# A long convolution's second transform in four 64x64 quarters of TensorE, and its spectral product taken from PSUM

## The chip, the cores and the metric

One core of a Trainium2 chip runs the whole kernel. The metric is the device time of one execution in microseconds (us); several executions are timed and the median is quoted. A core has five engines that work side by side, each through its own instructions in order: TensorE (PE, with its weight loads shown apart as PEld), VectorE (DVE), ScalarE (ACT), GpSimd (POOL) and SyncE (SP), which here issues nearly all DMA transfers. PE writes its results into PSUM, 8 banks of 128 partitions x 512 f32 numbers; DVE and ACT read them there. Semaphores make an engine wait for another.

## The reference, cut to what matters

The block has attention heads and Hyena heads side by side, then a mixture of experts. The Hyena part is what changes: a long convolution of length 2 x 2048 by FFT, twice (two orders), on 512 channels.

```
Hf = rfft(filters, n=2L)                      # per order, per channel, complex
z = v
for o, gate in enumerate((x1, x2)):
    Z = rfft(z, n=2L)
    y = irfft(Z * Hf[o], n=2L)[:L]            # complex product per frequency
    z = gate * (y + z * bias[o])
```

## The kernel before, in words

**Two sides.** `block_kernel` builds a left side (input projection, then attention) and a right side (filters, Hyena, a part of a later embedding), both as Python generators that yield a declared cost. `interleave` draws from the side that is behind by those costs, so the costs set the order in which instructions are handed over. The tile framework then sets each engine's order. As engines take their instructions in order, a matmul of the right side that waits also holds the left side's matmuls behind it.

**FFT in matmuls.** The transform of 4096 points is split in 128 x 32. Step one multiplies with a 128x128 matrix (`w1`) and writes to a DRAM scratch (`s_f` for filters, `s_z` for data); it is read back with other partitions (`zt`). Step two has 32 matrices of 128x128 (`w2[j]`), one matmul each for 128 channels. Each of these matrices is sparse: two residues (halves) with real and imaginary rows.

**Filter stage** (`stage_filter`), 8 rounds (2 orders x 4 channel blocks): `gen` makes 32 slices of a filter in 8 calls of 8 matmuls of 64x64x128 and DVE multiplies by a decay window; `norm` scales; `fft1` is step one (8 calls); `fft2` is step two (8 calls of 4 matmuls), whose results ACT copies from PSUM and SP stores to `h_f`, real and imaginary part twice each, as the product needs them. Three PSUM banks in rotation (`psm`, tag `pm`) serve all four.

**Hyena stage** (`stage_hyena`), pairs of channel blocks in turn: `step1` (step one), then `mid` 8 times per order and block: load `zt` and the filter `ab`, four matmuls with `w2` (L503), ACT copies the result to `zf` (L505), two DMAs swap its upper and lower 64 partitions into `zs` (L507, L508), because the real part needs the imaginary one; DVE multiplies both (L509, L510), POOL adds (L511), four matmuls go back with `wa` (L514), ACT copies (L516), SP stores to `t_z`. `back` reads `t_z`, multiplies with `wb` and the gate, and feeds `step1` of the second order. Two PSUM banks, `ph0` and `ph1`, serve these.

**Around it.** L149 to L151 are the input projection's matmuls, L210 and L213 its short convolution on DVE. In attention L725 makes scores for a maximum (DVE reduces it, L727), L790 and L793 are the scores, L803 is the product with v, L813 the sums of exponentials. When the Hyena and the embedding part (L1506 to L1524) have given back their PSUM, attention gets a further bank (`banks_free`, two units of attention later).

Of the kernel before, what the change touches and what calls it, by code (L numbers as in the profile page):

```python
# [8 lines left out]
F32 = mybir.dt.float32  # L9
# [5 lines left out]
ALU = mybir.AluOpType  # L15
AX = mybir.AxisListType
PSUM = bass.MemoryType.PSUM

P = 128
# [264 lines left out]

TWO_PI = 2.0 * math.pi
# [7 lines left out]
def stage_filter(K, st, cns, consts, w_f1, b_f1, freq1, w_f2, b_f2, freq2, w_f3, bias, h_d, s_d):  # L293
# [5 lines left out]
    pc, psm = pool("fi_c", 1), pool("fi_p", 3, space=PSUM)  # L299
# [4 lines left out]
    H2 = (slice(0, 64), slice(64, 128))  # L304
# [8 lines left out]
    zr = pc.tile([1, P], F32, name="zr")  # L313
    nc.vector.memset(zr, 0.0)
# [46 lines left out]
    def gen(o, b, st):  # L361

        cs = slice(b * P, (b + 1) * P)
        st["g"], part = [], pw.tile([P, 8, P], F32, tag="part", name="part", bufs=1)
        st["part"] = part
        for q in range(8):
            dec = pw.tile([P, 4, P], F32, tag="dec", name="dec")
            nc.sync.dma_start(dec, decay_c[:, q * 4:q * 4 + 4, cs])
            ps = psm.tile([P, 512], F32, tag="pm", name="ps")
            hs = H2[q % 2]  # L370
            for i in range(4):
                for d_ in range(2):
                    nc.tensor.matmul(ps[d_ * 64:(d_ + 1) * 64, i * P:(i + 1) * P],
                                     h2[hs, q // 2 * 4 + i, d_ * 64:(d_ + 1) * 64], w3[hs, o, d_, cs],
                                     start=True, stop=True, skip_group_check=True)
            gq = pw.tile([P, 4, P], F32, tag="g", name="g", bufs=GB)
            nc.vector.tensor_tensor(out=gq, in0=ps.rearrange("p (a c) -> p a c", a=4), in1=dec, op=ALU.mult)
            nc.vector.tensor_reduce(out=part[:, q], in_=gq.rearrange("p a c -> p c a"), axis=AX.X, op=ALU.add,
                                    apply_absolute_value=True)
            st["g"].append(gq)  # L380
            yield 0.8
# [49 lines left out]
    def fft2(o, b):  # L431
        for q in range(8):
            js = slice(q * 4, q * 4 + 4)
            zt = pw.tile([P, 4, P], F32, tag="z2", name="zt")
            nc.sync.dma_start(zt, s_d[o, b].rearrange("(j r) n c -> (r n) j c", r=4)[:, js])
            ps = psm.tile([P, 512], F32, tag="pm", name="ps")
            for i in range(4):
                nc.tensor.matmul(ps[:, i * P:(i + 1) * P], K.w2[:, q * 4 + i], zt[:, i], start=True, stop=True)
            hs = pw.tile([P, 4, P], F32, tag="hs", name="hs")
            nc.scalar.copy(hs, ps.rearrange("p (a c) -> p a c", a=4))  # L440
# [3 lines left out]
            if q == 0:  # L444

                nc.sync.dma_start(h_d[o, b, 64:65, 0, 0], hs[64:65, 0])
                nc.sync.dma_start(h_d[o, b, 0:1, 0, 1], zr)
                nc.sync.dma_start(h_d[o, b, 64:65, 0, 1], zr)
            yield 0.9
# [17 lines left out]
def stage_hyena(K, st, wa_c, uc_d, h_d, s_d, t_d, yh_d):  # L467
# [4 lines left out]
    wa = pc.tile([P, 32, P], F32, name="wa")  # L472
# [3 lines left out]
    ps_tile = lambda i: psa.tile([P, 512], F32, tag=f"ph{i}", name="ph")  # L476
    v4 = lambda t: t.rearrange("p (a c) -> p a c", a=4)
    fl = lambda t: t.rearrange("p a c -> p (a c)")
    H2 = (slice(0, 64), slice(64, 128))

    def step1(o, b, z, q):

        for i in range(2):
            ps = ps_tile(i)
            nc.tensor.matmul(ps, K.w1d[H2[i]], fl(z[H2[i]]), start=True, stop=True)
            sg = pw.tile([P, 4, P], F32, tag="s1", name="sg")
            nc.scalar.copy(sg, v4(ps))
            nc.sync.dma_start(s_d[o, b, :, q * 8 + i * 4:q * 8 + i * 4 + 4], sg)
# [6 lines left out]
    def mid(o, b, q):  # L495
        js = slice(q * 4, q * 4 + 4)
        zt = pw.tile([P, 4, P], F32, tag="zt", name="zt")
        nc.sync.dma_start(zt, s_d[o, b].rearrange("(j r) n c -> (r n) j c", r=4)[:, js])
        ab = pw.tile([P, 4, 2, P], F32, tag="ab", name="ab", bufs=HB)
        nc.sync.dma_start(ab, h_d[o, b, :, js])  # L500
        ps = ps_tile(0)
        for i in range(4):
            nc.tensor.matmul(ps[:, i * P:(i + 1) * P], K.w2[:, q * 4 + i], zt[:, i], start=True, stop=True)  # L503
        zf = pw.tile([P, 4, P], F32, tag="zf", name="zf")
        nc.scalar.copy(zf, v4(ps))  # L505
        zs = pw.tile([P, 4, P], F32, tag="zs", name="zs")
# [5 lines left out]
        ps = ps_tile(1)  # L512
        for i in range(4):
            nc.tensor.matmul(ps[:, i * P:(i + 1) * P], wa[:, q * 4 + i], zs[:, i], start=True, stop=True)  # L514
        sg = pw.tile([P, 4, P], F32, tag="s2", name="sg")
        nc.scalar.copy(sg, v4(ps))  # L516
        nc.sync.dma_start(t_d[o, b].rearrange("(j r) n c -> (r n) j c", r=4)[:, js], sg)

    def back(o, b, q):
        bt = pw.tile([P, 8, P], F32, tag="bt", name="bt")  # L520
# [3 lines left out]
        ps = ps_tile(q % 2)  # L524
# [14 lines left out]
    def block(b):  # L539
# [6 lines left out]
        for o in range(2):  # L546
            for q in range(8):
                mid(o, b, q)
                yield 1.8
# [19 lines left out]
def hyena_consts(K, pool, tmp, w1_c, w2_c, wb_c):  # L569
# [4 lines left out]
    K.w2 = pool.tile([P, 32, P], F32, name="w2")  # L574
# [4 lines left out]
    K.sgn = pool.tile([P, 1], F32, name="sgn")  # L579
    nc.vector.memset(K.sgn[0:64], -1.0)  # L580
    nc.vector.memset(K.sgn[64:128], 1.0)
# [26 lines left out]
class Attention:  # L608
# [4 lines left out]
    H2 = (slice(0, 64), slice(64, 128))  # L613
# [1056 lines left out]
def dft_consts():  # L1670
# [53 lines left out]
    w2 = np.ascontiguousarray(w2.transpose(1, 0, 2))  # L1724
    wa = np.ascontiguousarray(wa.transpose(1, 0, 2))
# [42 lines left out]
def block_kernel(tc, A, out):  # L1768
# [4 lines left out]
    h_f = dt("h_f", (2, 4, P, 32, 2, P))  # L1773
# [104 lines left out]
```

## Time and profile before

| | us |
|---|---|
| median of 3 runs | 3211.95 (3210.45 to 3221.18) |
| the profiled execution | 3218.25 |
| its span | 3216.5 |
| PE busy | 2973.7 (92%) |
| DVE busy | 2146.4 (67%) |
| ACT busy | 1401.8 (44%) |
| POOL busy | 1289.7 (40%) |

The profiled execution is 6.3 us above the median, so a sum made in its span is compared with 3218.25 and then moved down by 6.3 us. Busy time of an engine is the union of its instructions. An f32 matmul of the program appears as two records of MATMUL (and two of LDWEIGHTS), so that 8 matmuls are "x16". The form "64*64 64x128" is rows*columns of the array that the matmul uses, and the moving operand. The filter stage lies between 88 and 740 us, the Hyena between 745 and 1511 us.

### The profile page before, as it was taken

How to read it: one execution, taken by the hardware profiler on the slowest of the kernel's cores; microseconds unless marked ns; L12 is line 12 of the kernel's file. 1: busy time of each engine (PE TensorE's matmuls, PEld its weight loads, DVE VectorE, ACT ScalarE, POOL GpSimd, SP SyncE). 2: the span in 40 equal slices, each digit the busy share in tenths (PEclk: the TensorE clock that was granted, in tenths of full speed). 3: DMA queues.
4: the chain of work that ended last, by engine and by line, in shares of the span. 5: the costliest groups of instructions: out<-in, count | busy, mean ns of one | idle time of the engine just before them, and what ended most of it. 6: DMA issues, size and time to landing. Idle time of an engine off the chain costs nothing.

```text
span 3216.5 us, 46830 instructions
## 1 busy us (share of the span) xinstructions
PE 2973.7 (92%) x16505; PEld 2031.9 (63%) x16505; DVE 2146.4 (67%) x2837; ACT 1401.8 (44%) x2200; POOL 1289.7 (40%) x1138
## 2 busy tenths in 40 slices
PE   6989989899899999999899999989999999998897
PEld 5767777685645445354444378866667677675676
DVE  5775675735678768677777745366667676775655
ACT  3243343343344344443444422245556665664322
POOL 1333444424367657565687733101111121121443
PEclk8999989999899999998999999989999999999898
DMA  6468676787856667476100244287789888897553
GB/s 207 132 194 252 202 210 203 209 232 217 253 160 190 196 193 198 149 209 198 62 18 15 60 144 151 98 273 277 250 277 355 290 301 283 295 347 243 183 184 111
DMA packets 549838, 645.08 MB, mean 201 GB/s; under 512 B 68710, under 2 KB 372649, under 8 KB 549215
## 3 DMA queue, kind: packets, MB, share of 16 engines
q1 hardware_dynamic: 529486, 586.58, 57.6%
q0 software_dynamic: 20112, 55.47, 5.4%
q8 instruction: 131, 2.15, 0.3%
q14 instruction: 109, 0.89, 0.1%
HBM read 463.49 MB, written 161.58 MB: 194 GB/s over the span
## 4 chain that ended last, share of the span: by engine, by line
PE 59%; DMA 14%; DVE 10%; issue 4%; POOL 3%; ACT 2%; SPq 1%; DVEq 0%; POOLq 0%; ACTq 0%
PE po L803 5%; PE ps L1314 4%; PE ps L1315 4%; PE ps L1316 4%; PE pa L725 3%; PE pr L1320 3%; PE ps L790 3%; PE ps L793 3%; PE ps L149 2%; PE ps L151 2%; PE ps L150 2%; DMA zt<-s_f 2%; DMA zs<-zf 2%; PE ps L1380 2%; PE ps L1382 2%
## 5 line engine op out<-in xcount | busy, mean ns | idle before, releaser
L1298 DVE TENSOR_TENSOR wl<-raw,wh 128x1024 fp32r<-128x1024 f32 x384 | 463.4, 1223 | 195.3 <-ACT wh L1293 184.7
L1293 ACT CAST wh<-raw 128x1024 fp32r<-128x1024 f32 x384 | 399.0, 1051 | 268.9 <-PE ps L1316 94.6
L813 POOL TENSOR_TENSOR sums<-e,sums 128x512 f32<-128x512 f32 x306 | 427.6, 1412 | 103.3 <-ACT e L794 98.9
L794 ACT ACTIVATE e<-ps 128x512 f32<-128x512 f32 x512 | 291.3, 600 | 273.2 <-PE ps L793 232.8
L727 DVE TENSOR_REDUCE mx<-pa 128x1 f32<-128x512 f32 x512 | 330.8, 681 | 90.5 <-PE pa L725 89.6
L803 PE MATMUL po<-e,v 128*64 128x512 f32 x1024 | 291.4, 624 | 0.9 <-ACT e L794 0.9
L1393 POOL DMA_DIRECT2D y_d<-ob x64 | 36.0, 565 | 593.1 <-DVE ob L1392 350.0
L1314 PE MATMUL ps<-wh,xt 128*128 128x512 f32 (+4 forms) x512 | 212.6, 416 | 6.3 <-ACT wh L1293 6.2
L1315 PE MATMUL ps<-wl,xt 128*128 128x512 f32 (+4 forms) x512 | 206.5, 403 | 7.6 <-DVE wl L1298 7.6
L1316 PE MATMUL ps<-wh,xt 128*128 128x512 f32 (+4 forms) x512 | 202.6, 396 | 0.0
L725 PE MATMUL pa<-kst,q 128*128 128x512 f32 x352 | 144.1, 454 | 22.1 <-DVE mx L727 19.0
L149 PE MATMUL ps<-xh,wh 128*128 128x512 f32 x384 | 158.4, 412 | 1.4 <-ACT U L205 1.3
L151 PE MATMUL ps<-xh,wl 128*128 128x512 f32 x384 | 158.0, 411 | 0.5 <-DVE wl L143 0.5
L150 PE MATMUL ps<-xl,wh 128*128 128x512 f32 x384 | 156.7, 408 | 0.0
L790 PE MATMUL ps<-q,kst 128*128 128x512 f32 x352 | 153.6, 436 | 3.3 <-ACT e L794 2.5
L813 DVE TENSOR_TENSOR sums<-e,sums 128x512 f32<-128x512 f32 x110 | 132.1, 1208 | 26.7 <-ACT e L794 25.7
L793 PE MATMUL ps<-q,k 65*128 65x512 f32 x352 | 143.2, 407 | 2.2 <-DMA q<-mr 2.2
L725 PEld LDWEIGHTS pa<-kst,q 128*128 128x128 f32 x352 | 64.1, 192 | 126.1 <-DVE mx L727 68.6
L89 POOL TENSOR_TENSOR wl<-raw,wh 128x2048 fp32r<-128x2048 f32 (+1 forms) x26 | 103.1, 3968 | 98.4 <-ACT wh L139 90.1
L511 POOL TENSOR_TENSOR zs<-zs,ab 128x512 f32<-128x512 f32 x64 | 89.7, 1402 | 96.3 <-DVE zs L510 70.8
L1320 PE MATMUL pr<-raw,xr 128*32 128x128 f32 (+1 forms) x2112 | 125.5, 302 | 0.9 <-DVE ob L1396 0.9
L1314 PEld LDWEIGHTS ps<-wh,xt 128*128 128x128 f32 (+4 forms) x512 | 95.3, 186 | 44.8 <-issue 14.5
(384 smaller groups left out, 7167.1 us busy)
## 6 DMA issues: line engine op xcount, KB each, us to landing
raw<-in_w_gate_dram SPq DMA_DIRECT2D x128, 512.0 KB
raw<-in_w_up_dram SPq DMA_DIRECT2D x128, 512.0 KB
raw<-in_w_down_dram SPq DMA_DIRECT2D x128, 512.0 KB
h_f<-hs SPq DMA_DIRECT2D x256, 128.0 KB
ab<-h_f SPq DMA_DIRECT2D x64, 512.0 KB
raw<-in_w_in_dram SPq DMA_DIRECT2D x30, 1024.0 KB
xt<-in_x_dram SPq DMA_DIRECT2D x32, 512.0 KB
dec<-in_c_decay_dram SPq DMA_DIRECT2D x64, 256.0 KB
```

The source lines that it names most:

```text
L725: nc.tensor.matmul(pa, qh[:, t * P:(t + 1) * P], self.kst[g][:, q * 512:(q + 1) * 512], start=True, stop=True)
L727: nc.vector.tensor_reduce(out=mx[:, t, q:q + 1], in_=pa, axis=AX.X, op=ALU.max)
L790: mm = nc.tensor.matmul(ps, self.kst[g][:, ks], qh[:, ql_s[i]], start=True, stop=False)
L793: last = nc.tensor.matmul(ps, self.k1[g][:, ks], ql[:65, ql_s[i]], start=False, stop=True)
L794: nc.scalar.activation(out=pe[:, i], in_=ps, func=AF.Exp, scale=0.125)
L803: mm = nc.tensor.matmul(po[H2[i]], v[:, kt, g * 64:(g + 1) * 64], pe[:, i], start=(kt == 0), stop=(kt == NT - 1), skip_group_check=True)
L813: acc[j][1].tensor_tensor(out=sums[j], in0=pe[:, i], in1=src, op=ALU.add)
L1293: nc.scalar.copy(hi, raw)
L1298: nc.vector.tensor_tensor(out=lo, in0=raw, in1=hi.bitcast(F32), op=ALU.subtract)
L1314: nc.tensor.matmul(ps[:m], xt[:, k, 0, :m], hv[:, j], start=(k == 0), stop=False)
L1315: nc.tensor.matmul(ps[:m], xt[:, k, 0, :m], lv[:, j], start=False, stop=False)
L1316: nc.tensor.matmul(ps[:m], xt[:, k, 1, :m], hv[:, j], start=False, stop=(k == 7))
```

## The change

Step two and its way back are cut into 64x64 matrices. For each j the two residues' input rows (64 each) go to a 64-column result of their own, and odd j swap the halves, so that four consecutive matmuls use the four quarters of the array (`spread`). The result of input half h stands in bank h of a pair of banks. The result now holds the real part in 32 partitions and the imaginary part in the next 32. `h_f` is stored in this layout, real part twice and imaginary part twice, as rows of 1024 numbers. In `mid` DVE multiplies the PSUM pair with both parts of the filter and writes two products; their exchange and signs are in a doubled inverse matrix (`wa[:, i]`), whose two parts are summed in PSUM by 32 matmuls of 64x64 (`gather_back`). The copy `zf`, the swap by DMA, the signed product and the sum on POOL are gone. `mid` and `fft2` run 4 times on 8 j in place of 8 times on 4.

`gen` handles two slices at once in four quarters. PSUM: the filter stage has one single bank (`psm`) and one pair (`psd`) in place of three banks; the Hyena one pair (`ph`) in place of `ph0` and `ph1`. ACT's copies go over 1024 columns. The declared costs become 0.5 (gen, fft2) and 1.9 per `mid` call.

```
+def spread(nc, ps, w, src, q):
+    for jj in range(4):
+        for odd in range(2):
+            for h in range(2):
+                nc.tensor.matmul(ps[H2[(h + odd) % 2], h, jj * P:(jj + 1) * P], w[H2[h], q * 8 + jj * 2 + odd],
+                                 src[H2[h], jj * 2 + odd], start=True, stop=True, skip_group_check=True)
+def gather_back(nc, ps, w, src, q):
+    for jj in range(4):
+        for i in range(2):
+            for odd in range(2):
+                for h in range(2):
+                    at = (h + odd) % 2
+                    nc.tensor.matmul(ps[H2[h], at, jj * P:(jj + 1) * P], w[H2[at], i, q * 8 + jj * 2 + odd],
+                                     src[H2[at], i, h, jj], start=(i == 0), stop=(i == 1), skip_group_check=True)
...
-    pc, psm = pool("fi_c", 1), pool("fi_p", 3, space=PSUM)
+    pc, psm, psd = pool("fi_c", 1), pool("fi_p", 1, space=PSUM), pool("fi_d", 1, space=PSUM)
...
     def fft2(o, b):
-        for q in range(8):
...
-            for i in range(4):
-                nc.tensor.matmul(ps[:, i * P:(i + 1) * P], K.w2[:, q * 4 + i], zt[:, i], start=True, stop=True)
...
-            for ab in range(2):
-                for half in range(2):
-                    nc.sync.dma_start(h_d[o, b, half * 64:(half + 1) * 64, js, ab], hs[ab * 64:(ab + 1) * 64])
...
+        for q in range(4):
...
+            spread(nc, ps, K.w2, zt, q)
...
+                        nc.sync.dma_start(h_d[o, b, u:u + 32, q, i], hs[r:r + 32].rearrange("p a c -> p (a c)"))
...
     def mid(o, b, q):
...
-        nc.scalar.copy(zf, v4(ps))
...
-        nc.sync.dma_start(zs[0:64], zf[64:128])
-        nc.sync.dma_start(zs[64:128], zf[0:64])
-        nc.vector.tensor_tensor(out=ab[:, :, 0], in0=ab[:, :, 0], in1=zf, op=ALU.mult)
-        nc.vector.scalar_tensor_tensor(out=zs, in0=zs, scalar=K.sgn, in1=ab[:, :, 1], op0=ALU.mult, op1=ALU.mult)
-        nc.gpsimd.tensor_tensor(out=zs, in0=zs, in1=ab[:, :, 0], op=ALU.add)
...
+        if q == 0:
+            nc.sync.dma_start(ab[32:33, 0, :P], h_d[o, b, 32:33, q, 1, :P])
+            for r in (0, 32):
+                nc.gpsimd.memset(ab[r:r + 1, 1, :P], 0.0)
+        ps = banks()
+        spread(nc, ps, K.w2, zt, q)
+        for i in range(2):
+            nc.vector.tensor_tensor(out=ab[:, i], in0=ab[:, i], in1=fl(ps), op=ALU.mult)
+        ps = banks()
+        gather_back(nc, ps, wa, ab.rearrange("p i (h j c) -> p i h j c", h=2, j=4), q)
```

Three places show what this does to PE's order. In the programs' names L295 is `spread`, L308 `gather_back`, L505 `step1`, L545 `back` after the change; L503, L514, L485 and L526 were these before. Attention's L725, L790, L793, L803 are L741, L806, L809, L819 after, and `gen` L373 is L395.

PE in the filter stage before, one round of its calls:

```order
L423 MATMUL ps<-gh,w1h 128x512
L424 MATMUL ps<-gh,w1l 128x512
L425 MATMUL ps<-gl,w1h 128x512
L438 MATMUL ps<-zt,w_552 128x128 x4
L373 MATMUL ps<-w_200,h_199 64x128 x8
```

PE in the filter stage after, at the end of a round:

```order
L295 MATMUL pd<-zt,w_553 64x128 x16
L448 MATMUL ps<-gh,w1h 128x512
L449 MATMUL ps<-gh,w1l 128x512
L295 MATMUL pd<-zt,w_553 64x128 x16
L450 MATMUL ps<-gl,w1h 128x512
```

A call of `spread` now stands for two of L438; two that use the one pair `pd` stand here with two matmuls between them.

PE in the middle of the Hyena before, from the first product of a `mid` to the second:

```order
L503 MATMUL ph<-zt,w_552 128x128 x4
L725 MATMUL pa<-kst_6422,qh 128x512 x2
L790 MATMUL ps<-q_6647,kst_6422 128x512
L793 MATMUL ps<-q_6647,k_6423 128x512
L725 MATMUL pa<-kst_6422,qh 128x512
L790 MATMUL ps<-q_6647,kst_6422 128x512
L793 MATMUL ps<-q_6647,k_6423 128x512
L803 MATMUL po<-e,v 64x512 x2
L514 MATMUL ph<-zs,wa 128x128 x4
```

The same after:

```order
L295 MATMUL ph<-zt,w_553 64x128 x16
L841 MATMUL pa<-sums,sel 32x512 x3
L841 MATMUL pa<-osq,sel 32x512
L741 MATMUL pa<-kst_6461,q_9336 128x512
L806 MATMUL ps<-q_8439,kst_6461 128x512
L741 MATMUL pa<-kst_6461,q_9336 128x512
L809 MATMUL ps<-q_8439,k_6462 128x512
L806 MATMUL ps<-q_8439,kst_6461 128x512
L809 MATMUL ps<-q_8439,k_6462 128x512
L819 MATMUL po<-e,v 64x512 x2
L741 MATMUL pa<-kst_6461,q_9336 128x512
L308 MATMUL ph<-ab,wa 64x128 x32
```

About one step of attention still stands between the two products; half as many pairs of them are left.

PE at the end of the Hyena before:

```order
L526 MATMUL ph<-bt,wb 64x512 x4
L825 MATMUL pa<-osq,sel 32x512
L725 MATMUL pa<-kst_7662,qh 128x512 x4
L526 MATMUL ph<-bt,wb 64x512 x2
L725 MATMUL pa<-kst_7662,qh 128x512 x10
L1506 MATMUL pt<-ident,pr 128x128 x2
L725 MATMUL pa<-kst_7662,qh 128x512
L1521 MATMUL pp<-plh,ph 128x512
L1522 MATMUL pp<-pll,ph 128x512
```

PE at the end of the Hyena after:

```order
L741 MATMUL pa<-kst_7903,q_12580 128x512 x3
L295 MATMUL ph<-zt,w_553 64x128 x16
L741 MATMUL pa<-kst_7903,q_12580 128x512 x2
L308 MATMUL ph<-ab,wa 64x128 x32
L295 MATMUL ph<-zt,w_553 64x128 x16
L308 MATMUL ph<-ab,wa 64x128 x32
L295 MATMUL ph<-zt,w_553 64x128 x16
L308 MATMUL ph<-ab,wa 64x128 x32
L545 MATMUL ph<-bt,wb 64x512 x16
L1522 MATMUL pt<-ident,pr 128x128 x2
L1537 MATMUL pp<-plh,ph 128x512
L1538 MATMUL pp<-pll,ph 128x512
```

The last calls of `mid` and all eight of the last `back` stand after one another with hardly any attention between them; before, attention filled this place. It comes after 224 of attention's 512 matmuls with v (L803, L819 after), before after 288.

## Rows read from the trace of the kernel before

**Rows 1.** The page: busy us of each engine, share, instructions.

```profile
PE 2973.7 (92%) x16505; PEld 2031.9 (63%) x16505; DVE 2146.4 (67%) x2837; ACT 1401.8 (44%) x2200; POOL 1289.7 (40%) x1138
```

**Rows 2.** Stretch, busy us of PE, PEld, DVE, ACT, POOL; clock, DMA share, GB/s.

```profile
88.00:760.00 672.00, 604.36 (x3957) 497.84 (x3956) 428.06 (x483) 245.52 (x403) 266.60 (x262) 0.94 0.72 208
760.00:880.00 120.00, 100.70 (x462) 71.21 (x460) 69.95 (x104) 43.52 (x81) 34.55 (x45) 0.87 0.76 228
880.00:1480.00 600.00, 561.95 (x2551) 292.45 (x2548) 466.99 (x618) 260.86 (x484) 399.43 (x290) 0.99 0.64 185
...
1500.00:1540.00 40.00, 32.47 (x97) 16.89 (x93) 20.71 (x35) 12.12 (x20) 4.40 (x4) 0.79 0.54 168
...
1600.00:1800.00 200.00, 198.01 (x774) 93.70 (x772) 158.81 (x231) 91.36 (x162) 158.35 (x119) 1.00 0.07 16
```

**Rows 3.** The chain of waits by line, 880 to 1480 us.

```profile
by line: PE po L803 12.4%; PE pa L725 8.2%; DMA zs<-zf 7.3%; issue 7.1%; PE ps L790 6.9%; PE ps L793 5.8%; PE ph L503 4.2%; PE ph L514 3.7%; DVE mx L727 3.5%; DVE ab L509 3.3%; DMA ab<-h_f 3.2%; PE ph L485 3.0%; PE ph L526 2.9%; DVE sums L8
```

**Rows 4.** Timeline of PE near 309 us: start, length, line, form, count.

```profile
308.62 0.40 PE L150 MATMUL ps<-xl,wh 128*128 128x512 f32 x1
308.86 0.39 PE L151 MATMUL ps<-xh,wl 128*128 128x512 f32 x1
309.17 1.09 PE L373 MATMUL ps<-w,h 64*64 64x128 f32 x16
310.19 0.50 PE L423 MATMUL ps<-gh,w1h 128*128 128x512 f32 x1
```

**Rows 5.** Timeline of PE near 2489 us, four column quarters of 32.

```profile
2489.62 1.30 PE L1320 MATMUL pr<-raw,xr 128*32 128x128 f32 x40
2490.85 0.50 PE L1315 MATMUL ps<-wl,xt 128*128 128x512 f32 x1
```

**Rows 6.** Both products of `mid` in the timeline of PE near 1190 us.

```profile
1190.36 1.05 PE L514 MATMUL ph<-zs,wa 128*128 128x128 f32 x8
1191.26 1.06 PE L503 MATMUL ph<-zt,w 128*128 128x128 f32 x8
1192.07 0.48 PE L790 MATMUL ps<-qh,kst 128*128 128x512 f32 x1
```

**Rows 7.** `step1` in the timeline of PE, near 750 and near 920 us.

```profile
749.53 1.12 PE L485 MATMUL ph<-z,w1d 64*128 64x512 f32 x2
750.58 0.66 PE L220 MATMUL pt<-ident,acc 128*128 128x128 f32 x4
751.17 1.12 PE L485 MATMUL ph<-z,w1d 64*128 64x512 f32 x2
...
919.88 1.13 PE L485 MATMUL ph<-z,w1d 64*128 64x512 f32 x4
920.94 0.50 PE L725 MATMUL pa<-kst,qh 128*128 128x512 f32 x1
```

**Rows 8.** Lines by themselves: duration ns minimum/median/maximum, first and last start.

```profile
L509 DVE TENSOR_TENSOR ab<-ab,zf x64: 674/772/6849, 805.7 to 1459.2; 128x512 f32<-128x512 f32 x64
L510 DVE SCALAR_TENSOR_TENSOR zs<-zs,sgn,ab x64: 734/752/2817, 810.0 to 1470.3; 128x512 f32<-128x512 f32 x64
L511 POOL TENSOR_TENSOR zs<-zs,ab x64: 1262/1278/1747, 810.8 to 1471.2; 128x512 f32<-128x512 f32 x64
L528 DVE TENSOR_TENSOR z<-ph,gt x32: 672/688/692, 917.0 to 1510.6; 128x512 f32<-128x512 f32 x32
L505 ACT COPY zf<-ph x64: 567/587/616, 804.9 to 1456.7; 128x512 f32<-128x512 f32 x64
```

**Rows 9.** What PE waited for, 880 to 1480 us: total us, times, longest.

```profile
PE pa L725 <- DVE mx L727: 20.0, 17, 2.4
```

**Rows 10.** DMA issues on SP that read or write `h_f`, ns as in rows 8.

```profile
L443 SPq DMA_DIRECT2D h_f<-hs x256: 574/620/1846, 209.3 to 739.5; - x128
L500 SPq DMA_DIRECT2D ab<-h_f x64: 319/338/1958, 746.9 to 1454.7; - x64
```

**Rows 11.** Chain of waits, 1480 to 1540 us: a piece's start, us, what.

```profile
1500.88 5.43 DMA bt<-t_z
```

More of the change, by code (lines that the diff above doesn't have):

```diff
@@ L365, in gen @@
         st["part"] = part
-        for q in range(8):
[L367 to L370, printed above, removed]
-            for i in range(4):
[L372 to L381, printed above, removed]
+        for q in range(0, 8, 2):
+            ps = psd.tile([P, 2, 512], F32, tag="pd", name="pd")
+            for i in range(4):
+                for hs, n in zip(H2, range(2)):
+                    for d_ in range(2):
+                        nc.tensor.matmul(ps[d_ * 64:(d_ + 1) * 64, n, i * P:(i + 1) * P],
+                                         h2[hs, q // 2 * 4 + i, d_ * 64:(d_ + 1) * 64], w3[hs, o, d_, cs],
+                                         start=True, stop=True, skip_group_check=True)
+            for n in range(2):
+                dec = pw.tile([P, 4, P], F32, tag="dec", name="dec")
+                nc.sync.dma_start(dec, decay_c[:, (q + n) * 4:(q + n) * 4 + 4, cs])
+                gq = pw.tile([P, 4, P], F32, tag="g", name="g", bufs=GB)
+                nc.vector.tensor_tensor(out=gq, in0=ps[:, n].rearrange("p (a c) -> p a c", a=4), in1=dec, op=ALU.mult)
+                nc.vector.tensor_reduce(out=part[:, q + n], in_=gq.rearrange("p a c -> p c a"), axis=AX.X, op=ALU.add,
+                                        apply_absolute_value=True)
+                st["g"].append(gq)
+                yield 0.5
     def norm(o, b, st):
@@ L475, in stage_hyena @@
     yhv = yh_d.rearrange("(a n) c -> a n c", n=32)
-    ps_tile = lambda i: psa.tile([P, 512], F32, tag=f"ph{i}", name="ph")
+    banks = lambda: psa.tile([P, 2, 512], F32, tag="ph", name="ph")
     v4 = lambda t: t.rearrange("p (a c) -> p a c", a=4)
     fl = lambda t: t.rearrange("p a c -> p (a c)")
-    H2 = (slice(0, 64), slice(64, 128))
     def step1(o, b, z, q):
+        ps = banks()
         for i in range(2):
[L484 to L488, printed above, removed]
+            nc.tensor.matmul(ps[:, i], K.w1d[H2[i]], fl(z[H2[i]]), start=True, stop=True)
+        sg = pw.tile([P, 8, P], F32, tag="sg", name="sg", bufs=3)
+        nc.scalar.copy(fl(sg), ps.rearrange("p a c -> p (a c)"))
+        nc.sync.dma_start(s_d[o, b, :, q * 8:q * 8 + 8], sg)
     def load2(t, part, b, q):
@@ L495, in mid @@
     def mid(o, b, q):
[L496 to L504, printed above, removed]
@@ new lines, in mid @@
+        ps = banks()
+        spread(nc, ps, K.w2, zt, q)
+        for i in range(2):
+            nc.vector.tensor_tensor(out=ab[:, i], in0=ab[:, i], in1=fl(ps), op=ALU.mult)
+        ps = banks()
+        gather_back(nc, ps, wa, ab.rearrange("p i (h j c) -> p i h j c", h=2, j=4), q)
+        sg = pw.tile([P, 2, 4, P], F32, tag="sg", name="sg", bufs=3)
+        nc.scalar.copy(sg.rearrange("p u j c -> p (u j c)"), fl(ps))
+        for u in range(2):
+            nc.sync.dma_start(t_d[o, b].rearrange("(j u r) n c -> u (r n) j c", u=2, r=4)[u][:, q * 4:q * 4 + 4],
+                              sg[:, u])
@@ L523, in back @@
         load2(gt, 1 + o, b, q)
-        ps = ps_tile(q % 2)
+        ps = banks()[:, 0]
         for i in range(2):
@@ L546, in block @@
         for o in range(2):
-            for q in range(8):
+            for q in range(4):
                 mid(o, b, q)
-                yield 1.8
+                yield 1.9
             yield from parts_in(2 + o)
@@ L573, in hyena_consts @@
     K.w1d = pool.tile([P, P], F32, name="w1d")
-    K.w2 = pool.tile([P, 32, P], F32, name="w2")
+    K.w2 = pool.tile([P, 32, 64], F32, name="w2")
     K.wb = pool.tile([P, 64], F32, name="wb")
@@ L612 @@
     half = staticmethod(lambda a, i: a.rearrange("p t (b h x) -> p t b h x", b=2, h=2)[:, :, :, i])
-    H2 = (slice(0, 64), slice(64, 128))
+    H2 = H2
     UT = (slice(0, NT // 2), slice(NT // 2, NT))
@@ L1723, in dft_consts @@
     wa[0, 80:96, 32:64] = -2 * np.sin(t64[:, :16]).T
-    w2 = np.ascontiguousarray(w2.transpose(1, 0, 2))
-    wa = np.ascontiguousarray(wa.transpose(1, 0, 2))
+    b2, ba, order = np.zeros((128, 32, 64), f64), np.zeros((128, 32, 64), f64), np.zeros(128, int)
+    for j in range(32):
+        for h in range(2):
+            at = (h + j) % 2
+            rows, out = slice(h * 64, h * 64 + 64), np.r_[h * 32:h * 32 + 32, 64 + h * 32:96 + h * 32]
+            b2[rows, j] = w2[j, rows][:, out]
+            ba[at * 64:at * 64 + 64, j] = wa[j, out][:, rows]
+            r = (j // 2 * 4 + at * 2 + h) * 2
+            order[r:r + 2] = 4 * j + 2 * h, 4 * j + 2 * h + 1
+    bj = ba.reshape(2, 2, 32, 32, 64)
+    bj = np.stack([bj[:, 1], -bj[:, 0]], 1).reshape(128, 32, 64)
+    w2, wa, wb = b2, np.ascontiguousarray(np.stack([ba, bj], 1)), wb[order]
     f = np.float32
@@ L1772, in block_kernel @@
     qkv_d, uc_d = dt("qkv_d", (S, 768)), [dt(f"uc_d{i}", (S, 512)) for i in range(3)]
-    h_f = dt("h_f", (2, 4, P, 32, 2, P))
+    h_f = dt("h_f", (2, 4, P, 4, 2, 1024))
     s_f, s_z, t_z = (dt(n, (2, 4, P, 32, P)) for n in ("s_f", "s_z", "t_z"))
```

44 lines of the change are left out of this document (17 added, 27 removed).

## Prediction

> **What bounds the kernel now.** I read the busy times first: PE is busy for 92% of the span, DVE for 67% [rows 1]. Then the stretches, since a share of the whole hides stages [rows 2]. In the filter stage (88 to 760 us) PE is busy 604 of 672 us at a granted clock of 0.94; in the first part of the Hyena (760 to 880) 101 of 120; where Hyena runs beside attention (880 to 1480) 562 of 600; where attention runs alone (1600 to 1800) 198 of 200. So PE is the bound in all of them, most purely where no Hyena work is left, and everything from 1860 us on is untouched by the change. Third the chain of waits of 880 to 1480 [rows 3]: PE's lines lead, but the swap DMA (zs<-zf) holds 7.3% of it, 44 us, and DVE's lines some more. A change here pays through PE's work, and through waits that hold PE in its order.
>
> **PE's work in quarters.** The cost of one call in 64x64 form is read from `gen`: 16 records start at 309.17 and the next line at 310.19, so 1.02 us with the turns into and out of this form; the 16 records go in pairs, since they share the rows and differ in columns [rows 4]. Four at a time is not shown for this form. Two neighbours bound it. With 32-column tiles, 40 records of L1320 take 1.23 us (2489.62 to 2490.85), 31 ns each, a rate that only several side by side give [rows 5], as one of 128 columns alone takes 0.1 us (0.81 for eight) [rows 6]. With two halves of rows, `step1`'s four records take 1.06 us together (919.88 to 920.94), as long as two alone (749.53 to 750.58) [rows 7]; so different rows, in different banks, run side by side too. I take four at a time.
>
> `gen`: 64 calls of 1.02 become 32 of 1.02, -33 us. `fft2` and the first product of `mid`: a call now is 8 records of 128x128, 0.81 us (L503) to 0.90 us (L514), 0.85 in the mean [rows 6], so 64 calls are 54 us; after, 32 calls of 32 records in quarters, 1.02 us each, are 33. That is -21 us for each of the two. The way back: 64 calls, 54 us; after, 32 calls of 64 records, 16 steps of four, 1.02 + 0.87 = 1.89 us each, 60: +6 us. `step1`: 11 of its 32 calls stand apart as the first one does (749.53 and 751.17 [rows 7]); both matmuls now wait for one pair of banks and start together, 11 x 1.05 = -12 us (0 to -34).
>
> Sum -81 us: -54 in the filter stage, which is -57 at its clock of 0.94, and -27 in the Hyena. If row halves did not overlap, `gen` would gain nothing, a `spread` would take 1.89 (+6 us for each of the two), the way back 32 x 3.6 = 115 (+61), `step1` nothing: +73 us. These are the two ends.
>
> The Trainium skill (TensorEngine Tiling (Array Packing), Key Properties) says that a change of tiling mode drains TensorE. The trace agrees in size: the 16 records' own steps are about 0.87 of the 1.02 us. It adds no term, since the 1.02 us hold the turn.
>
> **DVE, ACT, POOL.** The new products read 1024 columns from PSUM. Nearest row: 512 columns from PSUM with one operand from SBUF, 0.688 us [rows 8]; twice that is 1.38, with a fixed part 1.2; I take 1.3. 64 of them are 83 us. Gone are 64 x (0.772 + 0.752) = 98 us by medians (more by means: contention), 64 POOL sums of 1.278 = 82 us, 64 copies `zf` of 0.587 = 38 us. Other copies only merge. Off the path these give nothing directly; PE waits 20.0 us for DVE's maximum in 880 to 1480 [rows 9], of which I count a third back: -6 us. It could be 0 to -20.
>
> **DMA and SP.** 128 swaps go, with their 44 us on the chain [rows 3]. PE often had other work in these waits, as only 38 us of 600 are idle, so I count -10 us (0 to -25). `h_f` keeps its bytes and its 256 stores, but in rows of 4 KB: an issue takes 0.620 us now, and a load with such rows 0.338 [rows 10], so SP is freed of up to 72 us in the filter stage; loads of `zt` issue sooner and are half as many. I count -8 us (0 to -20). The one row more and two memsets for q = 0 happen 8 times, behind a load that was issued well ahead: nothing, or 8 us if not hidden.
>
> **What is added: waits on single buffers.** Each place that had rotating banks has one pair now.
>
> In the filter stage `gen` and `fft2` take turns on one pair. `gen` frees it after two products of about 0.69 us (as L528 [rows 8]) and a reduction, `fft2` after a copy of 1024 columns, about 1.1 us (twice 0.587 less a fixed part). In most turns twenty matmuls of the projection lie between, 5 us at the 0.24 from 308.62 to 308.86 [rows 4]: hidden. In the order some 20 of 64 turns have under 1.5 us between, as in the place shown, where the next `spread` stands two matmuls behind. At 0.8 us each: +15 us (5 to 40).
>
> In the middle of the Hyena about ten of attention's matmuls stand between the two products of a `mid`, 2.3 us at 0.24 each. They must cover 2 x 1.3 us on DVE and what stands ahead in its queue (the maxima L727 and the sums L813). Short by 0.5 us in 24 of the 32: +12 us (-5 to 50). Behind a waiting `gather_back` on PE stand attention's scores, and ACT waits for these. In the Hyena's first part the order is as dense before as after, and PE idles 19 of 120 us [rows 2]: +5 us (-10 to 20).
>
> At the end of the Hyena, before, three late `back` calls and long runs of L725 fill the wait for attention's further bank; PE idles 7.5 us in 1500 to 1540 [rows 2]. After, about 5.5 calls of `mid` stand in a row, each a chain of 1.02 + 2.6 + 1.89 + 1.1 = 6.6 us, of which 2.9 is PE's own; with 13 L741 (3 us) to fill, PE idles 5.5 x 3.7 - 3 = 17 us. Then comes a trip through DRAM like the 5.43 us of bt<-t_z [rows 11], eight `back` at 1.0 + 0.7 (5.5 idle), and the embedding's weights, which are loaded only when the Hyena's space is free (8 us, an estimate from the same 5.43 us and two copies of 1.1). That is 36 us, less the 7.5 of before, and some microseconds more as the clock falls in such a stretch (0.79 there): +35 us (15 to 60).
>
> **Sum.** -57 - 27 - 6 - 10 - 8 + 15 + 12 + 5 + 35 = -41 us. 3218.25 - 41 = 3177 for a profiled execution; 6.3 less in the median: 3171. The new waits have the weakest rows, and their upper ends are farther off than the lower, so I move to 3178.
>
> **Rivals.**
> First, the full PE gain, and the hold-ups melt: DVE and POOL are so much freer that products start at once, and the Hyena's end overlaps better than its order suggests. -57 - 27 - 20 - 25 - 15, with +10 for the end and +15 elsewhere, is -119: 3093; half of the further gain, 3130. For it: attention alone keeps PE at 99% [rows 2]. Against it: the row of `mid` at the end is in the order.
>
> Second, the single PSUM pair becomes the bound. Its places are between the two products of a `mid`, and between `gen` and `fft2`; its price is the stall of each. Against the gain of 57 + 27 + 6 + 10 + 8 = 108 us stand 40 us for the Hyena's two ends, so it decides from 68 us of stalls, as 1.2 us in each of 32 `mid` and 0.5 in each of 64 turns of the filter's pair. With 2.0 and 0.8 us it is 64 + 51 + 40 = 155, +47 in sum: 3259. For it: no buffer is spare, and PE keeps its order. Against it: most turns have 2 to 5 us between.
>
> The Trainium skill (TensorEngine Tiling (Array Packing), PSUM Bottleneck) warns of this: packing makes TensorE faster and not the emptying of PSUM. The rows agree that a pair takes PE 1.02 us to fill and DVE 2.6 to empty.
>
> Third, quarters do not overlap: +73 of PE and 67 of waits less 24 is +116: 3328. Against it stand the rows with two halves and with four columns side by side [rows 4, 5, 7]. Fourth, the gain is spent in waits to nothing that can be told: 3212.
>
> **How the numbers follow.** A measurement of this kernel tells 0.3% (10 us) from no change, so the bounds are 3202 and 3222. Forecast (3150 to 3205) 0.45; the first rival 0.17, the second 0.25, the third 0.04, the fourth 0.09. Faster: the first rival and nearly all of the forecast, 0.60. Within 0.3%: the fourth and the edges of the others, 0.13. Slower: most of the second, and the third, 0.27. The range takes in the lesser half of the first rival and the second up to near its price: 3115 to 3245. The forecast's own range is 3150 to 3205.
>
> **What would show it.** In the profile after: 32 records of `spread` from start to next line in about 1.0 us, 64 of `gather_back` in 1.9 (quarters; 1.9 and 3.6 would refute them). DVE's 128x1024 products near 1.3 us. PE's waits for DVE ab at `gather_back` and for ACT at `spread` below 1 us in the mean; more speaks for the second rival. The stretch from the last `spread` of the Hyena to the embedding's last matmul with PE idle for 30 us or more. The filter stage shorter by about 50 us, and no swap on the chain. The forecast is wrong if attention alone, after the Hyena, does not keep its pace, or if a stage beyond 1860 us changes.

## The result, and the profile after

The changed kernel takes 3181.05 us (median of 4, 3178.03 to 3189.39), the kernel before 3216.56 (median of 4 beside it): a ratio of 0.9893, interval 0.987 to 0.9916. The forecast was 3178. The profiled execution of after took 3189.39 us with a span of 3187.4, 29.1 us less than the span before.

The page of after, the row that answers to [rows 1]:

```profile
PE 2893.6 (91%) x19065; PEld 1942.2 (61%) x19065; DVE 2088.4 (66%) x2770; ACT 1357.0 (43%) x2040; POOL 1186.7 (37%) x1090
```

PE works 80.1 us less (2973.7 - 2893.6), yet the span is only 29.1 shorter: PE is idle for 51 us more (293.8 in place of 242.8). So the question is where these 51 us lie. Stretches of after, columns as in [rows 2], cut where the stages now begin and end (filter stage; start, middle and end of the Hyena; attention alone; the rest):

```profile
88.00:692.00 604.00, 530.77 (x4419) 428.88 (x4420) 435.48 (x486) 237.29 (x369) 265.29 (x262) 0.95 0.76 227
...
692.00:842.00 150.00, 111.73 (x1050) 75.48 (x1050) 75.10 (x101) 39.09 (x60) 25.93 (x46) 0.83 0.68 214
842.00:1286.00 444.00, 424.00 (x3051) 203.81 (x3050) 310.48 (x434) 182.34 (x303) 238.12 (x193) 0.98 0.61 181
1286.00:1396.00 110.00, 62.19 (x732) 35.06 (x730) 42.32 (x60) 13.47 (x18) 8.97 (x7) 0.68 0.65 182
...
1396.00:1830.00 434.00, 415.71 (x1584) 192.19 (x1585) 317.99 (x437) 199.74 (x357) 320.06 (x231) 0.98 0.12 36
```

The same stages in the kernel before:

```profile
745.00:895.00 150.00, 130.46 (x592) 89.25 (x590) 93.75 (x132) 56.40 (x104) 60.09 (x62) 0.90 0.77 232
895.00:1405.00 510.00, 477.50 (x2134) 243.15 (x2134) 390.29 (x526) 220.34 (x408) 330.50 (x241) 0.99 0.63 184
1405.00:1515.00 110.00, 102.29 (x453) 53.49 (x453) 88.33 (x117) 43.82 (x80) 68.44 (x50) 0.95 0.72 205
1515.00:1862.00 347.00, 328.63 (x1234) 152.91 (x1234) 253.26 (x338) 157.34 (x280) 247.51 (x178) 0.96 0.14 42
```

Length less PE's busy time is its idle time. At the Hyena's end it goes from 7.7 to 47.8 us (+40), at its start from 19.5 to 38.3 (+19), in its middle from 32.5 to 20.0 (-12); in attention alone it is 18 us in both kernels. The clock at the end is 0.68, in the kernel before 0.95. I call this end, where calls of the Hyena stand one behind the other, the clump. At the start PE's longest wait is for a load of `step1`'s input, which cost it nothing before; of the waits of after, 692 to 842 us (us in all, times, longest):

```profile
PE ph L505 <- DMA z<-uc_d: 10.7, 2, 8.0
```

What stands at the end is seen in PE's timeline of after (start, length, line, form, count, idle time before and what ended it); L295 is `spread`, L308 `gather_back`, L545 `back`, L1522 the embedding:

```profile
1336.92 3.95 PE L308 MATMUL ph<-ab,wa 64*64 64x128 f32 x64 [2.52 <-issue]
1342.02 1.99 PE L295 MATMUL ph<-zt,w 64*64 64x128 f32 x32 [1.15 <-ACT sg L533]
1346.53 3.51 PE L308 MATMUL ph<-ab,wa 64*64 64x128 f32 x64 [2.52 <-issue]
1351.21 1.08 PE L545 MATMUL ph<-bt,wb 128*64 128x512 f32 x4 [1.17 <-ACT sg L533]
1358.92 1.98 PE L545 MATMUL ph<-bt,wb 128*64 128x512 f32 x4 [6.63 <-DMA bt<-t_z]
...
1384.43 1.97 PE L545 MATMUL ph<-bt,wb 128*64 128x512 f32 x4 [2.88 <-DMA bt<-t_z]
1395.98 0.66 PE L1522 MATMUL pt<-ident,pr 128*128 128x128 f32 x2 [9.58 <-DMA pr<-in_p_dram]
```

The reader should see the chain of a `mid` without cover: 2.5 us for DVE's two products before every L308, 1.15 us for ACT's copy before every L295, and calls that take nearly twice their usual time (3.5 to 4.0 us where the same call takes 1.9), as the clock has fallen towards its lower level (0.59 in 1340 to 1360). In the middle of the Hyena a call reads like this (1.98 us listed, 1.90 to the next start):

```profile
1114.87 1.98 PE L308 MATMUL ph<-ab,wa 64*64 64x128 f32 x64
1116.77 0.96 PE L741 MATMUL pa<-kst,q 128*128 128x512 f32 x3
...
1120.24 1.10 PE L295 MATMUL ph<-zt,w 64*64 64x128 f32 x32
1121.28 0.50 PE L741 MATMUL pa<-kst,q 128*128 128x512 f32 x1
```

So 32 records take 1.04 us and 64 take 1.90, the numbers that the prediction gave for four quarters side by side. DVE's products from PSUM take 1.21 us:

```profile
L529 DVE TENSOR_TENSOR ab<-ab,ph x64: 1201/1214/1223, 752.8 to 1345.2; 128x1024 f32<-128x1024 f32 x64
```

### The profile page after: what moved, and what is told of

Same layout as the page of the kernel before. It is cut to its first block, busy times and chain, and to the rows that moved or that the text cites. A ratio compares the mean times of both kernels' runs of the same rounds, so it can differ in the third digit from the quotient of the medians.

```text
span 3187.4 us, 50724 instructions
## 1 busy us (share of the span) xinstructions
PE 2893.6 (91%) x19065; PEld 1942.2 (61%) x19065; DVE 2088.4 (66%) x2770; ACT 1357.0 (43%) x2040; POOL 1186.7 (37%) x1090
## 5 line engine op out<-in xcount | busy, mean ns | idle before, releaser
L829 POOL TENSOR_TENSOR sums<-e,sums 128x512 f32<-128x512 f32 x306 | 411.0, 1359 | 156.5 <-ACT e L810 152.1
L819 PE MATMUL po<-e,v 128*64 128x512 f32 x1024 | 293.8, 627 | 3.5 <-ACT e L810 3.5
L741 PE MATMUL pa<-kst,q 128*128 128x512 f32 x352 | 142.0, 454 | 18.3 <-DVE mx L743 12.9
L806 PE MATMUL ps<-q,kst 128*128 128x512 f32 x352 | 151.7, 431 | 0.0
L829 DVE TENSOR_TENSOR sums<-e,sums 128x512 f32<-128x512 f32 x110 | 123.9, 1133 | 35.4 <-ACT e L810 34.8
L809 PE MATMUL ps<-q,k 65*128 65x512 f32 x352 | 142.0, 403 | 4.8 <-DMA q<-mr 4.8
L741 PEld LDWEIGHTS pa<-kst,q 128*128 128x128 f32 x352 | 63.6, 193 | 121.9 <-DVE mx L743 66.8
L1279 POOL DMA_INDIRECT g<-h_d,idx x52 | 70.0, 1347 | 140.1 <-PE pt L1288 58.6
```

The costliest lines, as they stand in the source:

```text
L741: nc.tensor.matmul(pa, qh[:, t * P:(t + 1) * P], self.kst[g][:, q * 512:(q + 1) * 512], start=True, stop=True)
L819: mm = nc.tensor.matmul(po[H2[i]], v[:, kt, g * 64:(g + 1) * 64], pe[:, i], start=(kt == 0), stop=(kt == NT - 1), skip_group_check=True)
L829: acc[j][1].tensor_tensor(out=sums[j], in0=pe[:, i], in1=src, op=ALU.add)
```

## The experiments

Theory: PE's work is less by what was forecast, the single pair of banks costs nothing in the middle, and a clump of uncovered calls at the Hyena's end takes much of it back. Rivals: the pair is the bound; quarters do not matter, as PE is not; attention's pace sets the end, and the clump is no loss.

**1. The clump taken apart.** Attention's further bank is asked for two units later; in the order its matmuls then stand between the last calls of `mid`.

```
-BANKS_AFTER = 2
+BANKS_AFTER = 4
```

> The changed kernel, with attention's further PSUM bank taken four units of attention after Hyena and embedding are done in the order of emission instead of two. In the order the calls at the Hyena's end then stand 10 to 15 attention matmuls apart again, and the embedding comes after 280 of attention's 512 products with v instead of 224. Theory (the clump at the Hyena's end costs about 40 us of idle PE, the attention work stands ready to fill it, and that work is not missed later): PE idle from 1300 us to the embedding falls from 48 us to under 15, the granted clock there stays above 0.9, and the time is 3150 (3138 to 3162). Rival A (the idle time only moves: attention's softmax on ACT and DVE sets its pace, so the units drawn forward leave PE waiting elsewhere): 3172 to 3185, with PE's idle time over the whole span unchanged. Rival B (a later further bank slows attention itself by more than the clump cost): above 3185.

Measured: 3110.06 us, ratio to before 0.9667 (0.9651 to 0.9682): 71 us less than after, over twice the 31 that the theory expected. The Hyena's end, attention alone, and 1350 to 1400 us in this run, and then 1350 to 1400 us of after:

```profile
1300.00:1413.00 113.00, 105.16 (x825) 52.51 (x824) 84.17 (x115) 44.02 (x75) 62.38 (x48) 0.98 0.62 174
1413.00:1754.00 341.00, 334.37 (x1280) 154.02 (x1279) 264.08 (x363) 162.28 (x286) 255.56 (x183) 0.99 0.14 39
...
1350.00:1400.00 50.00, 45.87 (x226) 19.30 (x223) 37.20 (x57) 15.42 (x26) 22.52 (x17) 0.97 0.65 178
```

```profile
1350.00:1400.00 50.00, 18.50 (x46) 4.75 (x43) 8.74 (x12) 3.85 (x5) 0.00 (x0) 0.53 0.75 207
```

PE's idle time at the end falls from 47.8 to 7.8 us, in attention alone from 18.3 to 6.6, and PE's busy time over the span by 28.5 us (2893.6 to 2865.1) for the same 19065 records. Of these 28.5, `gather_back` has 10.1, `back` 6.1, `spread` 1.5 and the embedding's L1522 and L1537 to L1539 3.8 (each record counted up to the next one's start): 21.5 us in calls that stood in the slow stretch or at its end. The other 7 are spread over other lines; the part of the program behind attention alone, which the clump doesn't reach, was itself 7 us shorter (1350.0 us here, 1357.4 in after). The spans of the two profiled executions differ by 83.4 us, 12 more than the medians: 40 of idle time at the end, 11.7 in attention, 28.5 of busy time, and some 3 elsewhere. Rivals A and B fall: PE's idle time over the span goes from 293.8 to 238.9 us and comes back nowhere.

**2. The same clump in the kernel before.** A call of its `mid` declares half as much, so that a block's calls declare what they do after the change:

```
-                yield 1.8
+                yield 0.95
```

> The kernel before with one number changed: a call of its mid declares 0.95 instead of 1.8, so that a block's calls declare in sum what they do after the change. In the order about eleven of its calls then stand in a row at the Hyena's end and the embedding comes after 224 products with v, as after the change. Theory (the clump comes from the declared costs and the moment at which the further bank is asked for, not from the single PSUM pair or the quarters): PE idle in the last 120 us ahead of the embedding rises from 7 us to 40 or more, and the time to 3275 (3250 to 3310). Rival (with its two single banks in rotation the kernel before has calls that overlap, and gets through such a row): 3210 to 3235.

Measured: 3288.96 us, ratio 1.0221 (1.018 to 1.0262). Two stretches ahead of the embedding:

```profile
1385.00:1435.00 50.00, 32.01 (x147) 28.41 (x146) 14.46 (x20) 10.26 (x18) 13.05 (x11) 0.64 0.84 242
1435.00:1485.00 50.00, 21.89 (x51) 6.98 (x51) 9.26 (x13) 4.96 (x8) 0.00 (x0) 0.53 0.74 213
```

PE is idle for 46 us of 100 and the clock is down to 0.53, without pair and quarters, and the time lies in the theory's range: the clump comes from the declared costs against the moment of the bank. Two banks in rotation did not save it. The other way round, the kernel before with the bank later:

> The kernel before with the further PSUM bank taken four units later instead of two, nothing else. Theory (the clump came with the change, whose Hyena is over earlier; before, PE is idle for only 7 us in the 107 us ahead of the embedding): 3217 (3207 to 3222), no difference that can be told. Rival (taking the bank later is good by itself, attention runs faster with its work in this order): 3190 to 3205.

Measured: 3201.87 us, 0.9945 (0.9925 to 0.9966). The theory missed here, and the number lies in the rival's range. The span is 16.5 us shorter, 10 of it PE's busy time and 6 its idle time. I read this as a small clump that before had too (7.5 us idle at a clock of 0.79 in 1500 to 1540 [rows 2]); that a later bank is good by itself is not excluded here, but in experiment 3, where no clump is left, it gains nothing.

**3. Another remedy.** In the changed kernel `yield 1.9` behind a `mid` becomes 3.6, the bank stays at two units.

> The changed kernel with the declared cost of a call of mid doubled-up to 3.6, about what two calls of before declared, and the bank left at two units. In the order the Hyena is drawn more slowly, its last calls stand 7 to 12 attention matmuls apart, and the embedding comes after 282 products with v. Theory (it is the clump that costs, whatever removes it): 3112 (3102 to 3124). Rival (what helped was the late bank): it is taken here where it stood in the other run, so the same; rival B (the Hyena drawn slower ends later and holds back the last stage, or its first calls lose their cover): 3130 to 3180.

Measured: 3091.33 us, 0.9607 (0.9583 to 0.963), the fastest of all, 90 us under after and 11 under the theory's range. Its stretches, and then the first two of experiment 1:

```profile
694.00:844.00 150.00, 120.58 (x1085) 77.58 (x1085) 83.20 (x114) 43.15 (x67) 31.56 (x50) 0.84 0.72 222
844.00:1300.00 456.00, 443.08 (x3408) 216.35 (x3408) 329.19 (x468) 191.59 (x322) 256.90 (x203) 1.00 0.64 188
1300.00:1413.00 113.00, 109.94 (x738) 55.73 (x735) 84.93 (x126) 46.32 (x82) 61.55 (x46) 1.00 0.53 151
```

```profile
694.00:844.00 150.00, 111.62 (x1075) 72.36 (x1073) 81.58 (x110) 42.78 (x66) 27.24 (x48) 0.87 0.73 225
844.00:1300.00 456.00, 433.89 (x3223) 209.60 (x3220) 317.96 (x441) 185.52 (x309) 243.14 (x196) 0.98 0.60 177
```

Slower drawing also takes 9 us of idle time out of the start (38.4 to 29.4, against experiment 1) and 9 out of the middle (22.1 to 12.9). Both remedies together:

> The kernel with the slower declared costs (3091), and the further bank taken two units later as well. No calls stand in a row in either order. Theory (the bank's moment matters only by the clump that it makes): 3091, within 8 us. Rival (a later bank is good or bad for attention by itself): outside 3083 to 3100.

Measured: 3104.37 us, 0.9636 (0.96 to 0.9672). That is 13 us more, outside the theory's 8; but the intervals overlap, so whether the later bank costs anything here is not settled. It gains nothing.

**4. Is the pair the bound?** One more DVE operation in each `mid`:

```
+        nc.vector.tensor_tensor(out=ab[:, 1], in0=ab[:, 1], in1=ab[:, 1], op=ALU.max)
```

> The changed kernel with one more DVE operation in each call of mid, behind the two products and ahead of the way back: the second product's 128x1024 result against itself (maximum), which changes no value and takes about 1.2 us. Theory (attention's matmuls between the two products cover DVE with room to spare in the middle of the Hyena; only the dense calls at the start and the end, some 10 of 32, show it): +12 us, 3193 (3185 to 3201). Rival (the single pair is the bound, every call's chain through DVE is exposed): 32 x 1.2 = +38, 3219.

Measured: 3231.58 us, 1.0032 (1.0016 to 1.0048), 50 more, beyond the rival's number. But its order had changed: eight calls of `mid` now stood in a row at the end, and in the 200 us ahead of the embedding PE was idle for 86 us against 48 in after. So the same operation again without a clump (the bank at six units, in experiment 1 at four):

> The further DVE operation of 1.2 us in each call of mid again, but with attention's further PSUM bank taken six units later, so that in the order no calls at the Hyena's end stand in a row. Compared with the run that only takes the bank later (3110). Theory (attention's matmuls cover DVE's part of mid everywhere but in the first eight, dense calls; the 50 us that the same operation cost before were a longer clump at the end, whose idle PE time was 38 us more): 3122 (3112 to 3135). Rival (the single PSUM pair is the bound in every call): 32 x 1.2 us more, 3148 or above.

Measured: 3115.81 us, 0.9696 (0.9671 to 0.9721), 6 us over experiment 1, with overlapping intervals, for 32 x 1.2 = 38 us of DVE. Not all of the 38 stood in PE's way, as the timeline with the same operation shows (the first run of this experiment):

```profile
1327.14 0.70 PE L308 MATMUL ph<-ab,wa 64*64 64x128 f32 x8 [2.56 <-DVE ab L529]
1328.31 3.26 PE L308 MATMUL ph<-ab,wa 64*64 64x128 f32 x56 [0.46 <-DVE ab L530]
```

PE begins 8 of the 64 records ahead of the operation, the others 1.17 us later. At 1.90 us for 64 the 8 take some 0.24 us, so a call's chain grows by some 0.9 us (an estimate); 32 of these are 30 us, and 6 were seen. The Hyena's pair is not the bound. In the middle of the fastest kernel (844 to 1400 us) PE's longest waits are (us in all, times, longest):

```profile
PE pa L741 <- DVE mx L743: 8.8, 9, 1.9
PE ph L545 <- DMA bt<-t_z: 4.0, 3, 1.8
PE ph L308 <- issue: 1.2, 1, 1.2
PE ph L308 <- DVE ab L529: 1.0, 1, 1.0
```

The Trainium skill (TensorEngine Tiling (Array Packing), PSUM Bottleneck) says that after packing has made TensorE four times as fast, the copy out of PSUM may become the bottleneck. The trace agrees where nothing stands between the calls (2.5 us before each L308 of the clump), and not where attention does (2.2 us before all L308 in 844 to 1400 us of the fastest kernel).

The filter's pair `pd` was in no experiment. In 88 to 692 us of after PE's waits at it add up to 11.4 us; of these 2.0 are for DVE and ACT that empty it, and 6.5 have no cause in the profile. The rival had 51.

**5. What are the quarters worth?** The same products, one row half after the other, so that mostly column neighbours meet (in `gather_back` likewise):

```
-    for jj in range(4):
-        for odd in range(2):
-            for h in range(2):
+    for h in range(2):
+        for jj in range(4):
+            for odd in range(2):
```

> The changed kernel with the same 64x64 products in another order in both new functions: all of one row half first, then all of the other, so that neighbours in the order share rows and only two of the four quarters can work together. Theory (four quarters work together now, and PE's time is the bound wherever these calls stand): a call of 32 records takes 1.9 us instead of 1.03, one of 64 records 3.6 instead of 1.9; 64 x 0.87 + 32 x 1.75 = 112 us more PE, and the time rises by nearly all of that: 3281 (3255 to 3300). Rival (the emptying of the PSUM pair by DVE and ACT is the bound, and PE's part lies beside it): less than half, under 3235. If the order does not matter to the overlap: 3181.

Measured: 3236.49 us, 1.0057 (1.0035 to 1.0078), 55 more than after. Timeline of PE:

```profile
1130.01 1.59 PE L295 MATMUL ph<-zt,w 64*64 64x128 f32 x32
1131.53 1.05 PE L841 MATMUL pa<-osq,sel 128*32 128x512 f32 x2
...
1136.29 3.34 PE L308 MATMUL ph<-ab,wa 64*64 64x128 f32 x64
1139.56 0.96 PE L741 MATMUL pa<-kst,q 128*128 128x512 f32 x3
```

The calls take 1.52 and 3.27 us (1.9 and 3.6 were expected), so 64 x 0.49 + 32 x 1.36 = 75 us were added. They are shorter than expected because by the records' starts the second row half begins 0.50 us after the first, and the two run side by side for four of their eight steps in the call of 32. Without the clump:

> Products in column pairs again (a call of 32 records takes 1.52 us in place of 1.03, one of 64 takes 3.27 in place of 1.91: 64 x 0.49 + 32 x 1.36 = 75 us more PE), now with the further bank taken later. Theory (without the clump PE is the bound in the Hyena as well, and the filter stage has some slack): 3110 + 44 + 16 for the Hyena and half of 16 for the filter stage, 3178 less 8, 3170 (3158 to 3185). Rival (PE has slack everywhere, as the 6 us for 16 us of PE in the generation alone seemed to say): under 3150.

Measured: 3153.06 us, 0.9806 (0.9785 to 0.9827): 43 over experiment 1. And the generation alone (the loops over row halves and over `i` exchanged):

> The changed kernel with only the generation of the filters in pairs of columns again: one row half first, then the other. Theory (the filter stage is bound by PE): 32 calls x 0.87 us = 28 us, divided by the clock of 0.95 for part of it: 3210 (3203 to 3216). Rival (the filter stage is bound by the exchange of its single PSUM pair, whose waits grow as each fill takes longer in turns that stand close): more than 40 us, 3222 or above. Rival (the filter stage is bound by transfers or DVE, and PE's time there is hidden): under 3192.

Measured: 3187.08 us, 0.9899 (0.9881 to 0.9917): 6 more, with overlapping intervals, in the range of its second rival (under 3192), for some 15 us of PE (`gen` 51.1 us in place of 35.9). In 88 to 696 us PE is busy for 543.95 us there and for 534.12 in after, in a stage of the same length. So a microsecond added to PE's calls costs 43/75, some 0.6, in the Hyena and filter together, and some 6/15, within the noise, in the filter stage alone. The first run's 3236 lies just above its rival's "under 3235" and far from the theory's 3255, the second's 3153 between rival and theory; in the generation alone the rival, that PE's time is hidden, has the number.

**6. Rows and swap.** On the kernel of experiment 3, `h_f` laid out in rows of 128 numbers again:

```
-    h_f = dt("h_f", (2, 4, P, 4, 2, 1024))
+    h_f = dt("h_f", (2, 4, P, 4, 8, 2, P))
```

> The kernel with the slower declared costs (3091), with the filter's spectrum laid out so that its rows in DRAM are 128 numbers again instead of 1024: as many store issues (256) and loads (32), each with eight times as many pieces; DVE and PE read the same numbers in another order of columns. Theory (the longer rows freed SP and the queues, and the waits for zt<-s_f, 18 us before and 1 after in the filter stage, went with them): an issue takes 0.62 us again instead of 0.42, and the time is 10 to 20 us longer, 3106. Rival (SP is idle enough in the filter stage that its issues do not matter): 3088 to 3096.

Measured: 3102.6 us, 0.9648 (0.96 to 0.9695), 11 more with overlapping intervals: not settled. An issue's median is 0.578 us against 0.423, so the mechanism is there; the wait for zt<-s_f rose only to 3.5 us. In the profiled executions `step1` first runs at 706.7 us in place of 694.9, as the theory has it, but that is one execution of each. Then the copy and the DMAs back in `mid`, on the kernel of experiment 3 with the bank two units later as well (the lines that come in):

```
+        nc.scalar.copy(zf, fl(ps))
+        nc.sync.dma_start(zs[0:64], zf[0:64])
+        nc.sync.dma_start(zs[64:128], zf[64:128])
+        nc.vector.tensor_tensor(out=ab[:, 0], in0=ab[:, 0], in1=zf, op=ALU.mult)
+        nc.vector.tensor_tensor(out=ab[:, 1], in0=ab[:, 1], in1=zs, op=ALU.mult)
```

> The kernel with the slower declared costs, with the old way from the first product to the spectral product put back: ACT copies the PSUM pair to SBUF, two DMAs copy that (here onto the same partitions, so no value changes place), and DVE multiplies the one and the other copy with the two parts of the filter. The further bank is taken two units later still, so that no calls stand in a row at the end. Per call the chain gets some 1.0 us of ACT and 2 to 3 us of DMA longer; in the order 15 to 17 attention matmuls stand between the two products in place of 13 to 15. Theory (attention covers most of this in the middle; the gain from the exchange in the weights is mainly that a wait behind a DMA is gone in the dense calls): 3091 + 20 = 3111 (3100 to 3130). Rival (the exchange by DMA is hidden anyway, its removal gave nothing): 3088 to 3097. Rival (the chain through the swap is the bound of the Hyena): 32 x 3.5 us, above 3160.

Measured: 3201.29 us, 0.9939 (0.9915 to 0.9963), 110 more than experiment 3, and 97 more than the run with both remedies (3104.37), which has the bank at the same place. The theory's 3130 is passed, and the second rival's number (above 3160) is met. But both copies shared three buffers with the results, and 1550 to 1600 us shows 17 us of idle PE, a clump again, so the number holds more than the longer chain. PE's idle time in 800 to 1600 is 75 us, and of the waits (844 to 1500)

```profile
PE ph L308 <- DVE ab L534: 18.2, 10, 5.7
```

stands where the fastest kernel has 1.0. So nothing speaks for the first rival, a hidden exchange; but the runs do not part the exchange from the shared buffers and the clump, and what it cost before stays open.

## Why the prediction was right, point by point

**The time** was right to 3 us, but by luck: it is a sum of sizes that erred both ways.

**PE's work** was right. With each record counted up to the next one's start, `spread` (and L438, L503) went from 121.1 to 73.0 us (-48; forecast -42), `gen` from 72.1 to 35.9 (-36; -33), the way back from 60.1 to 75.3 (+15; +6, of which the clump's clock made 10), `step1` from 47.4 to 37.9 (-9.5; -12). In sum -79, forecast -81. The third rival (no overlap) is out by the calls of 1.04 and 1.90 us.

**That it counts in full** is borne out by one pair of runs and not by another. With the bank at four units in both kernels (experiments 2 and 1) the change takes 98 us from PE's busy time (2963.3 to 2865.1) and 96 from the span (3200.0 to 3104.0). But time added to the same calls costs only about 0.6 (experiment 5). Why the two differ was not tried.

**The clump** is the term that was mis-sized. Its place and its length (5.5 calls, eight `back`, the embedding's load) were as told from the order. Its idle time was 47.8 us where the forecast's pieces add up to 36, and its price was 71 by experiment 1, where +35 was forecast. The forecast counted "some microseconds more" for the clock; it was some 21 us of slower records, and there were 12 us of idle time in attention behind it.

**The waits on single buffers** were priced too high in the middle: +12 was forecast with -16 against it (swap, maxima), -12 was measured, and 38 us more of DVE cost 6. In the filter stage idle time rose from 67.6 (88 to 745) to 73.9 us (88 to 696), +6, near the forecast +15 less 8, but by other terms: PE's wait for zt<-s_f went from 18.0 to 1.4 us, the wait at the pair was under the 15, and PE's waits for step one's inputs (`gh` and `gl`) rose from 4.9 to 21.5. `step1` first runs at 695.9 us in place of 749.5, 54 earlier, forecast 50. **The Hyena's start** cost +19, not +5. The forecast looked only at how dense the calls stand there; the longest wait is `step1`'s for the load z<-uc_d, 10.7 us for which it had no term. The Hyena starts 54 us earlier than before; whether the load is late for that reason was not tried.

So, from before to after in the two profiled spans, the clump took 27 us more than forecast (40 idle and 21.5 of slower records, for 35) and the start 14 more. This was paid back in part by PE, which without those slower records works 102 us less than before where 84 were forecast, and by 8 us in the middle. The 12 us in attention don't count here, as the kernel before lost them as well. The span fell by 29 us where the sum said 41; the last step of the forecast, from 3171 to 3178, made up for most of that. Some 10 of PE's 102 may be the small clump of before (experiment 2). Why the rest of PE's lines became faster was not tried.

**The rivals.** The second (the pair is the bound) is refuted for the Hyena by experiment 4, the DVE operation at +6 us; for the filter's pair there is only the sum of waits named there. The first (hold-ups melt, 3093) did not come true of the changed kernel. With slower drawing the kernel comes to 3091; that this is by the rival's terms is not shown. Against the kernel before with the bank later that is 3091.33/3201.87 = 0.9655, some 110 us; with the bank at four units in both it is 92 (3201.87 to 3110.06). Of this worth of the change the order of emission had hidden three fifths to two thirds.

## What to carry to other kernels

When a change makes calls cheaper, look again at the numbers by which they are drawn among other work, and at what waits for their buffers: with a declared cost of 3.6 instead of 1.9 the same instructions run 90 us faster. Look in the order for calls in a row with nothing between, and price them at the chain's full length with the work at half the clock. A microsecond of the busiest engine need not be worth a microsecond: here it was about 0.6 when calls were made longer, though the engine is busy for 92% of the span.

## What the runs showed of the hardware

A step of four quarters costs what a step of two column neighbours does. In `spread` after the change four records start within 0.02 us of each other and the next four 0.109 us later; in `gen` before, near 309 us, two records start together and the next two 0.109 us later. So 16 records in pairs took 1.02 us and 32 in quarters take 1.03. From 1.03 and 1.91 us for 8 and 16 steps, a step is 0.110 us and the turn into and out of the form some 0.15, an estimate. Rows of 4 KB instead of 512 bytes take SP's issue of a store of 128 KB from 0.578 to 0.423 us. And in the clump of after the granted clock falls to 0.50, its lower level of 1.2 GHz: it is 0.78 in 1300 to 1340 us, where PE is busy for 26.9 of 40 us, 0.59 in 1340 to 1360 (8.5 of 20) and 0.50 in 1360 to 1400 (16.3 of 40); it is 0.98 in 1400 to 1420, once the embedding's matmuls run one behind the other (16.3 of 20).
